# State space group in the memory and banks that the recurrence had; linear attention's states beside the recurrence

## The chip, the cores and the metric

One core of one Trainium2 chip runs the whole block. The metric is the device time of one execution, in microseconds (us). The kernel is written in a tile framework: a scheduler orders the instructions of each engine when the kernel is built, from the order of the program, the pools of memory and the banks; the order is then fixed. The engines are TensorE (PE), VectorE (DVE), ScalarE (ACT), GpSimd (POOL) and SyncE (SP, which issues nearly all DMAs).

## What is computed

One layer of a hybrid block on 1024 latent tokens with a prefix of 256 context tokens, width 1024. A normed input goes through one projection (`w_in`) into three mixers that run over the tokens in both directions; their outputs are joined and projected (`w_out`); a mixture of experts follows. The three mixers, cut to what matters here:

```python
def rwkv7_scan(r, w, k, v, a, b, s0):            # 4 heads of 64
    def step(s, inp):
        r_t, w_t, k_t, v_t, a_t, b_t = inp
        sa = jnp.einsum('bhvk,bhk->bhv', s, a_t)
        s = s * w_t[:, :, None, :] + sa[..., None] * b_t[:, :, None, :] + v_t[..., None] * k_t[:, :, None, :]
        return s, jnp.einsum('bhvk,bhk->bhv', s, r_t)
...
def ssd_chunked(x, dA, bm, cm, s0):              # 8 heads of 64, chunks of 128
    a_cs = jnp.cumsum(dA, -1)
    decay_in = jnp.exp(jnp.where(causal, a_cs[..., :, None] - a_cs[..., None, :], -jnp.inf))
    scores = jnp.einsum('bclhn,bcshn->bhcls', cm, bm) * decay_in
    y_diag = jnp.einsum('bhcls,bcshp->bclhp', scores, x)
    decay_to_end = jnp.exp(a_cs[..., -1:] - a_cs)
    states = jnp.einsum('bclhn,bhcl,bclhp->bchpn', bm, decay_to_end, x)
    ...
    y_off = jnp.einsum('bclhn,bchpn,bhcl->bclhp', cm, states[:, :-1], jnp.exp(a_cs))
    return y_diag + y_off
...
def gla_chunked(q, k, v, logg, s0):              # 4 heads, keys 32, values 64, chunks of 64
    b_cs = jnp.cumsum(logg, 2)
    att = jnp.einsum('bclhd,bcshd->bchls', q * jnp.exp(b_cs - ref), k * jnp.exp(ref - b_cs))
    o_intra = jnp.einsum('bchls,bcshe->bclhe', att, v)
    kv = jnp.einsum('bcshd,bcshe->bchde', k * jnp.exp(b_end[:, :, None] - b_cs), v)
    s_start = ...   # the running sum of kv over the chunks, decayed
    o_inter = jnp.einsum('bclhd,bchde->bclhe', q * jnp.exp(b_cs), s_start)
    return o_intra + o_inter
```

## The kernel before

The program goes through these stages. (1) To about 562 us: norm, `w_in` in column groups, the preparation of each mixer, and for the recurrence the inverse of a triangular matrix per chunk (`rw_inverse`). (2) The recurrence, in 20 steps of 64 tokens, both directions and all heads at once (`rw_step`, with `rw_out` one step behind). (3) The rest of the three mixers. (4) The output projection (`outproj`), the router, the experts.

**A step of the recurrence** (all its matmuls are 64x64, at line 596 in the helper `heads`, 16 to a group): `pa` from `cd`, `v` and the state `Z`; ACT copies it to `rh`; `pb` from `rh` and `sm`; ACT copies it to `u`; `pz` from `v`, then from `u`; DVE adds `pz` to `Zd` and gives the next `Z`; POOL makes `Zd`. `py`, the output, is summed from `cd` and `v`, `cd` and `Z`, `sm` and `u`, and ACT (p < 12) or DVE writes it to `y`. SP loads for every step `cd` (768 KB, two buffers), `sm` (line 582, and 585 from step 4 on) and two halves of `v` (line 588, three buffers). `pa`, `pb` and `pz` share the two banks `ch`, `py` has the one bank `rg`.

**GLA**: `gla_states` loads `vg`, transposes ten gate tiles (`ptg`), makes the decays (`la`, `cum`, `kend`) and sums the states (`ptk` transposes, `pkv` matmuls, `gS`); `gla_out` makes the scores (`pat`, line 881) and outputs (`po`, lines 904 and 907) in two groups, norms them (`gsq`, `pin`, `pbn`) and stores them to `mixD`.

**SSD**: `ssd_dt` makes the step sizes and their sums; each sum is split into three bfloat16 parts (`csp`), which go to `difD` in DRAM in 48 stores (lines 1056 to 1058). `ssd_states` goes through ten chunks: transposes `ptx` and `ptB`, weighting `xs` (one direction on DVE, the other on POOL), matmul `pss`, then the running sum `sacc`, `S` on POOL, stored to `stD`. `ssd_out` goes through eight tiles: `ssd_weights` builds the decay matrix `pe` from a mask and two products over `df` (lines 1135, 1137, 1139), `pa` (line 1149), `Cd` on POOL and the scores `pcb`; then `pyd` (line 1188), whose second operand `st` is a state loaded from `stD`.

`outproj_consts` splits `w_out` into `woh` and `wol` and makes small constants (`pgr`, `prb`); `outproj` makes `pso` in two halves for each of eight tiles. `rw_finish` norms the output of the recurrence (`pm`, `fs`, `pin`, `pbn`).

What sets the order: a stage can only run beside another if its pool of memory and its banks are open at the same time. Before, `ps2` (ch=2, rg=1) and `ps3` (sd=3, gl=2) are open from the recurrence to the projection, and the pools `sd` and `gl` lie on the right side, in memory that is free by then, so that the states of both GLA and SSD run beside the recurrence. The scheduler mixes them into the gaps.

## Time and profile before

| | us |
|---|---|
| three runs: median (lowest, highest) | 1535.78 (1533.09, 1540.34) |
| profiled execution | 1533.99 |
| its span, from first to last instruction | 1532.2 |
| last inverse ends, recurrence begins | about 562 to 572 |
| recurrence ends | about 738.5 |
| first pso of the projection | about 905 |
| last pso | about 1010 |
| PE busy in the span | 1340.5 (87%) |
| DVE, ACT, POOL busy | 785.2, 515.4, 389.5 |

The table gives where the stages lie in the profiled execution; busy shares of the whole span say little, since every stage has another limit. All the change's edits lie between 562 and 1010 us, but for the set-up of the fixed part of `difD`, which lies in the first stage. "SPq" in the trace is the time in which SP issues a DMA, not that of the transfer.

### The profile page before, as it was taken

To read this page: it belongs to the slowest core of one execution; us is meant where nothing else is said; L and a number is where in the kernel's file an instruction comes from. 1 tells how busy PE (TensorE), PEld (TensorE's weight loads), DVE (VectorE), ACT (ScalarE), POOL (GpSimd) and SP (SyncE) were. 2 spreads that over 40 slices of the span, in tenths; PEclk is the share of its full clock that TensorE was granted. 3 is DMA by queue.
4 is the path that set the end of the run, shared out by engine and by line. 5 is a ranking of instruction groups with operands and counts; after the bars stand their busy time and mean duration, and the time that the engine had idled before them with its cause. 6 is when DMAs were issued, how large, how long until landed. Compare 5 with 4: busy or idle time off the path is not lost. (4 is left out here: it accounts for less than half of the span.)

```text
span 1532.2 us, 28018 instructions
## 1 busy us (share of the span) xinstructions
PE 1340.5 (87%) x11077; PEld 1111.9 (73%) x11077; DVE 785.2 (51%) x1482; ACT 515.4 (34%) x1056; POOL 389.5 (25%) x432
## 2 busy tenths in 40 slices
PE   7897899999797776777889989993999999999984
PEld 3585677777676774666557767762999999999984
DVE  4849868889979854414564472227102212112532
ACT  5544334443363134422433352220212212212333
POOL 3312432343334111413453252112101111111112
PEclk9997899999899777889856589995999999999998
DMA  9454867677661467476544365425988868868984
GB/s 320 134 156 138 201 153 169 167 189 180 162 144 31 93 141 203 127 229 207 185 145 118 97 208 171 145 97 193 368 299 288 271 201 301 294 224 299 311 266 123
DMA packets 297253, 296.81 MB, mean 194 GB/s; under 512 B 114281, under 2 KB 214890, under 8 KB 297119
## 3 DMA queue, kind: packets, MB, share of 16 engines
q1 hardware_dynamic: 288095, 269.81, 57.7%
q0 software_dynamic: 7872, 20.97, 5.7%
q10 hardware_dynamic: 1152, 4.19, 0.7%
q8 instruction: 89, 1.46, 0.4%
q14 instruction: 45, 0.37, 0.1%
HBM read 221.44 MB, written 73.72 MB: 193 GB/s over the span
## 5 line engine op out<-in xcount | busy, mean ns | idle before, releaser
L1576 PE MATMUL p<-hT,w 128*128 128x144 f32 (+10 forms) x2048 | 263.2, 288 | 0.0
L1576 PEld LDWEIGHTS p<-hT,w 128*128 128x128 f32 x2048 | 257.6, 192 | 0.6
L262 PE MATMUL psi<-hlo,whi 128*128 128x512 f32 (+1 forms) x440 | 172.0, 391 | 5.0 <-DVE hlo L234 3.8
L261 PE MATMUL psi<-hhi,whi 128*128 128x512 f32 (+1 forms) x440 | 170.3, 389 | 0.0
L263 PE MATMUL psi<-hhi,wlo 128*128 128x512 f32 (+1 forms) x440 | 169.9, 387 | 0.3 <-POOL wlo L254 0.3
L1583 PE MATMUL p<-hid,w 128*128 128x144 f32 (+10 forms) x1024 | 136.6, 294 | 8.4 <-DVE hid L1578 7.2
L1583 PEld LDWEIGHTS p<-hid,w 128*128 128x128 f32 x1024 | 133.9, 199 | 9.0 <-DVE hid L1578 7.5
L1602 POOL DMA_INDIRECT acc<-yr,rows x27 | 41.4, 1532 | 323.0 <-DVE yr L1598 188.2
L1578 DVE TENSOR_TENSOR hid<-hid,p 128x144 f32<-128x144 f32 (+10 forms) x64 | 18.7, 294 | 170.0 <-PE p L1576 165.9
L262 PEld LDWEIGHTS psi<-hlo,whi 128*128 128x128 f32 x440 | 85.6, 195 | 26.0 <-DVE hlo L234 5.6
L263 PEld LDWEIGHTS psi<-hhi,wlo 128*128 128x128 f32 x440 | 85.4, 194 | 19.1 <-issue 3.4
L261 PEld LDWEIGHTS psi<-hhi,whi 128*128 128x128 f32 x440 | 85.8, 195 | 17.7 <-issue 2.1
L1598 DVE TENSOR_SCALAR yr<-pty,rows 128x512 f32<-128x512 f32 (+8 forms) x46 | 32.7, 741 | 112.4 <-PE pty L1592 105.2
L1584 ACT ACTIVATE yT<-p,mods 128x144 f32<-128x144 f32 (+10 forms) x128 | 43.0, 374 | 112.7 <-PE p L1583 112.5
L1577 ACT ACTIVATE hid<-p 128x144 f32<-128x144 f32 (+10 forms) x64 | 18.2, 284 | 168.8 <-PE p L1576 168.7
L739 DVE SCALAR_TENSOR_TENSOR co<-gr,pc,co 128x512 f32<-128x512 f32 x72 | 59.4, 849 | 6.5 <-ACT co L728 4.7
L190 DVE SCALAR_TENSOR_TENSOR aacc<-wada,csig,aacc 128x512 f32<-128x512 f32 x56 | 51.6, 921 | 15.6 <-DMA wada<-in_ada_w_dram 15.3
L262 PE MATMUL pso<-wol,mh 128*128 128x512 f32 x128 | 52.8, 412 | 3.3 <-DVE wol L1222 2.2
L261 PE MATMUL pso<-woh,mh 128*128 128x512 f32 x128 | 52.4, 412 | 1.0 <-DVE go L1265 1.0
L263 PE MATMUL pso<-woh,ml 128*128 128x512 f32 x128 | 52.6, 411 | 0.0
L463 PE MATMUL psg<-AR,BK 64*128 64x128 f32 x320 | 46.6, 304 | 4.0 <-DVE BK L456 1.6
L463 PEld LDWEIGHTS psg<-AR,BK 64*128 64x128 f32 x320 | 39.5, 204 | 13.4 <-issue 4.0
(540 smaller groups left out, 2668.3 us busy)
## 6 DMA issues: line engine op xcount, KB each, us to landing
w<-in_moe_w_dram SPq DMA_DIRECT2D x47, 2048.0 KB
wada<-in_ada_w_dram SPq DMA_DIRECT2D x32, 512.0 KB
cd<-stepD SPq DMA_DIRECT2D x20, 768.0 KB
wraw<-in_w_in_dram SPq DMA_DIRECT2D x24, 512.0 KB
aw<-in_ada_w_dram SPq DMA_DIRECT2D x10, 512.0 KB
stepD<-AR SPq DMA_DIRECT2D x40, 128.0 KB
mabD<-G SPq DMA_DIRECT2D x40, 128.0 KB
stepD<-G SPq DMA_DIRECT2D x40, 128.0 KB
```

The lines of the kernel that those rows point to most:

```text
L190: nc.vector.scalar_tensor_tensor(acc, w[:, k % 2], g.sg[:, k, 0:1], acc, op0=OP.mult, op1=OP.add)
L261: nc.tensor.matmul(ps, whi(k), xhi(k), start=k == 0, stop=False)
L262: nc.tensor.matmul(ps, whi(k), xlo(k), start=False, stop=False)
L263: nc.tensor.matmul(ps, wlo(k), xhi(k), start=False, stop=k == 7)
L463: nc.tensor.matmul(pg[h][:, c, :], bkf[HS[h], c], arf[HS[h], c], start=True, stop=True)
L739: nc.vector.scalar_tensor_tensor(o, src(dy, dx), w(3 * dy + dx), o, op0=OP.mult, op1=OP.add)
L1576: nc.tensor.matmul(p[:, 0:n], w[:, k, fs], hT[:, k, s0:s0 + n], start=k == 0, stop=k == 7)
L1578: nc.vector.tensor_mul(hid[:, f, 0:n], hid[:, f, 0:n], p3[:, 0:n])
L1583: nc.tensor.matmul(p[:, 0:n], w2[:, f, 128 * k:128 * k + 128], hid[:, f, 0:n], start=f == 0, stop=f == 3)
L1584: nc.scalar.activation(yT[:, k, 0:n], p[:, 0:n], AF.Copy, scale=g.mods[:, 40 + k, 0:1])
L1598: nc.vector.tensor_scalar(yr[0:m, h], pf, wt[0:m, b:b + 1], None, op0=OP.mult)
L1602: nc.gpsimd.indirect_dma_start(out=g.acc, out_offset=bass.IndirectOffsetOnAxis(ap=rows[0:m, 0, b:b + 1], axis=0), in_=yr[0:m, :], in_offse ...
```

## The change

It moves four things. The banks: beside the recurrence only GLA has banks of its own (gl=3), and the recurrence has ch=3 and rg=2; when it has ended, its banks become SSD's (sd=4, rg=1). The memory: `gl` and the new pool `yp` (with `y`, and the tiles of `rw_finish`) are on the right during the recurrence; SSD's pool `sd` takes the memory of `rw` on the left, so that no SSD work can start before the last step is done. The order of the program: GLA's states, the finish of the recurrence, SSD's step sizes, GLA's output, then SSD's states and output, with the projection's constants between the tiles. And the layout of `difD`: six rows of tiles instead of eight, the parts of two products stacked along the contraction (K from 36 to 48), so that the third `pe` matmul goes; the parts go to DRAM in one store (`partsD`), and 16 + 8 DMAs from there to `difD`. Tags of banks follow: `pm` and its norm to sd, `pyd` to rg, `pgr` and `prb` to gl, `pso` to sd, `pto` to gl. All eight banks are in use before (ch=2, rg=1, sd=3, gl=2), and in both new stages (ch=3, rg=2, gl=3; sd=4, rg=1, gl=3).

```diff
@@ -638,7 +638,7 @@
     if p == 4:
-        g.y = g.rw.tile([128, 2, TL], F, tag="y", name="y")
+        g.y = g.yp.tile([128, 2, TL], F, tag="y", name="y")
     py = py.rearrange("p (b d) t -> p b d t", b=2)
@@ -653,16 +653,16 @@
             ts = slice(t0, t0 + 512)
-            x = g.rw.tile([128, 1536], F, tag="cd", name="fw", bufs=2)
+            x = g.yp.tile([128, 1536], F, tag="fw", name="fw", bufs=2)
             yc, bv, gt = (x[:, 512 * i:512 * i + 512] for i in range(3))
-            sq = g.rw.tile([128, 512], F, tag="sm", name="fs", bufs=2)
+            sq = g.yp.tile([128, 512], F, tag="fs", name="fs", bufs=2)
             nc.sync.dma_start(bv, g.bvD[b, :, ts])
             nc.sync.dma_start(gt, g.gtD[b, :, ts])
-            pm = g.ps.tile([128, 512], F, tag="ch", name="pm")
+            pm = g.ps.tile([128, 512], F, tag="sd", name="pm")
             nc.tensor.matmul(pm, g.blk64, g.y[:, b, ts], start=True, stop=True)
...
             nc.scalar.activation(sq, yc, AF.Square)
-            pb = inv_norm(g, g.rw, "ch", sq, g.blk64[:, ::64], 1.0 / 64, 2)
+            pb = inv_norm(g, g.yp, "sd", sq, g.blk64[:, ::64], 1.0 / 64, 2)
             nc.vector.tensor_mul(yc, yc, pb)
@@ -949,17 +949,18 @@
     nc = g.nc
-    g.difD = g.dram.tile([8, 128, 8, 128], BF, name="difD")
-    t = g.tmp.tile([128, 8, 128], BF, tag="rv", name="dift", bufs=1)
+    g.difD = g.dram.tile([8, 128, 6, 128], BF, name="difD")
+    t = g.tmp.tile([128, 6, 128], BF, tag="rv", name="dift", bufs=1)
     nc.gpsimd.memset(t, 0.0)
...
         for h in range(4):
-            nc.sync.dma_start(t[o + 24 + 3 * h:o + 27 + 3 * h, h], g.oneb[0:3])
+            for r in (24, 36):
+                nc.sync.dma_start(t[o + r + 3 * h:o + r + 3 + 3 * h, h], g.oneb[0:3])
     nc.sync.dma_start(g.difD.rearrange("c p i t -> p c (i t)"),
-                      t.rearrange("p i t -> p (i t)")[:, None].to_broadcast([128, 8, 1024]))
+                      t.rearrange("p i t -> p (i t)")[:, None].to_broadcast([128, 8, 768]))
@@ -1048,14 +1049,17 @@
     nc.vector.tensor_scalar(parts[:, 2], parts[:, 0], -1.0, None, op0=OP.mult)
+
+    pD = g.dram.tile([3, 128, 3, 128], BF, name="partsD")
+    nc.sync.dma_start(pD.rearrange("k p i t -> p k (i t)"), parts.rearrange("p k i t -> p k (i t)"))
     for d in range(2):
...
             for h in range(4):
-                src = parts[64 * d + 4 * q + h:64 * d + 64:8]
-                o = 64 * q + 3 * h
-                nc.sync.dma_start(g.difD[:, o + 12 * d:o + 12 * d + 3, h], src[:, 0])
-                nc.sync.dma_start(g.difD[:, o + 24:o + 27, 4 + d], src[:, 2])
-                nc.sync.dma_start(g.difD[:, o + 24:o + 27, 6 + d], src[:, 1])
+                o = 64 * q + 12 * d + 3 * h
+                nc.sync.dma_start(g.difD[:, o:o + 3, h], pD[0, 64 * d + 4 * q + h:64 * d + 64:8])
+            for r, k in ((24, 2), (36, 1)):
+                nc.sync.dma_start(g.difD[:, 64 * q + r:64 * q + r + 12, 4 + d],
+                                  pD[k, 64 * d:64 * d + 64].rearrange("(c q h) i t -> q c (h i) t", q=2, h=4)[q])
@@ -1119,12 +1123,12 @@
     nc.sync.dma_start(xt, g.xsD[:, :, ts])
-    df = W.tile([128, 8, 128], BF, tag="df", name="df", bufs=2)
+    df = W.tile([128, 6, 128], BF, tag="df", name="df", bufs=2)
     nc.sync.dma_start(df, g.difD[tl - 2])
...
         nc.sync.dma_start(C2[HS[d]], g.xsD[:, 5, ts].rearrange("(g n) t -> n g t", g=2))
-    K = [slice(64 * q, 64 * q + 36) for q in range(2)]
+    K = [slice(64 * q, 64 * q + 48) for q in range(2)]
     R = [df[K[q], 0:4].rearrange("p h t -> p (h t)") for q in range(2)]
@@ -1134,9 +1138,7 @@
         for q in range(2):
-            nc.tensor.matmul(pe[q].rearrange("p h t -> p (h t)"), df[K[q], 4 + d], R[q], start=False, stop=False)
-        for q in range(2):
-            nc.tensor.matmul(pe[q].rearrange("p h t -> p (h t)"), df[K[q], 6 + d], R[q], start=False, stop=True)
+            nc.tensor.matmul(pe[q].rearrange("p h t -> p (h t)"), df[K[q], 4 + d], R[q], start=False, stop=True)
         for q in range(2):
@@ -1180,7 +1182,7 @@
         nc.gpsimd.tensor_mul(yz, xt[:, 0:4, :], g.dskip[:, :, None].to_broadcast([128, 4, 128]))
-        py = g.ps.tile([128, 4, 128], F, tag="sd", name="pyd")
+        py = g.ps.tile([128, 4, 128], F, tag="rg", name="pyd")
@@ -1209,7 +1211,7 @@
     for hf in range(2):
-        pg = g.ps.tile([128, 4, 128], F, tag="ch", name="pgr")
+        pg = g.ps.tile([128, 4, 128], F, tag="gl", name="pgr")
         for j in range(4):
@@ -1229,7 +1231,7 @@
     nc.sync.dma_start(rb[:, 4:20], dap(g.a["moe_re_b"], 0, [[0, 128], [1, 16]]))
-    pr = g.ps.tile([128, 512], F, tag="ch", name="prb")
+    pr = g.ps.tile([128, 512], F, tag="gl", name="prb")
     for k in range(8):
@@ -1258,13 +1260,13 @@
         for hf in range(2):
-            ps = g.ps.tile([128, 512], F, tag="ch", name="pso")
+            ps = g.ps.tile([128, 512], F, tag="sd", name="pso")
             h = slice(512 * hf, 512 * hf + 512)
...
             nc.gpsimd.tensor_add(x[:, h], x[:, h], go)
-            pt = g.ps.tile([128, 4, 128], F, tag="gl" if tl < 4 else "sd", name="pto")
+            pt = g.ps.tile([128, 4, 128], F, tag="gl", name="pto")
             for j in range(4):
@@ -1803,8 +1805,9 @@
     B.close("psm", "ps1")
-    B.open("left", "ps2", ch=2, rg=1)
-    B.open("right", "ps3", sd=3, gl=2)
+    B.open("right", "ps3", gl=3)
+    B.open("left", "ps2", ch=3, rg=2)
+    M.open("right", "yp", "gl")
     M.open("left", "rw")
@@ -1813,23 +1816,25 @@
     late()
-    rw_finish(g)
     M.close("rw")
-    M.open("right", "sd", "gl")
+    B.close("ps2")
+    B.open("left", "ps5", sd=4, rg=1)
+    M.open("left", "sd")
     g.vg = g.gl.tile([128, 10, 280], F, name="vg")
...
     gla_states(g)
+    rw_finish(g)
     ssd_dt(g)
+    gla_out(g)
+    M.close("gl", "yp")
+    M.open("right", "op")
     ssd_states(g)
     ssd_out(g, range(2, 6))
-    gla_out(g)
-    M.close("gl")
-    M.open("left", "op")
     outproj_consts(g)
...
     outproj(g)
-    M.close("op", "ab", "sd")
-    B.close("ps2", "ps3")
+    M.close("op", "sd", "ab")
+    B.close("ps5", "ps3")
     B.open("left", "ps4", mm=5, tp=3)
```

How the instructions of three places stand now. A number behind a name tells apart buffers of the same name; the pairs of the two halves of a head group are counted together (x8 stands for eight pairs).

PE, from `pb` of step 7 on, before; `cd_5637` is the load of step 7, `cd_5724` that of step 8:

```order
L596 MATMUL pb_5667<-rh_5665,sm_5639 64x64 x8
L596 MATMUL pz_5680<-v_5643,cd_5637 64x64 x8
L596 MATMUL py_5784<-cd_5637,Z_5655 64x64 x2
L859 MATMUL pkv_7043<-vg_6891,ke_7041 32x64 x4
L859 MATMUL pkv_7049<-vg_6891,ke_7041 32x64 x2
L596 MATMUL pz_5680<-u_5676,cd_5637 64x64 x8
L596 MATMUL pa_5733<-v_5730,cd_5724 64x64 x8
L596 MATMUL py_5784<-sm_5639,u_5676 64x64 x8
L596 MATMUL pa_5733<-Z_5742,cd_5724 64x64 x8
L859 MATMUL pkv_7049<-vg_6891,ke_7041 32x64 x2
L849 MATMUL ptk_7055<-ident_85,kend_7006 128x128
L596 MATMUL py_5871<-cd_5724,v_5730 64x64 x8
```

PE at the same place in the changed kernel, from the row ahead of `pb` of step 7 on; `cd_5651` is the load of step 7 there, `cd_5738` that of step 8:

```order
L596 MATMUL py_5885<-cd_5738,v_5744 64x64 x5
L596 MATMUL pb_5681<-rh_5679,sm_5653 64x64 x8
L596 MATMUL pz_5694<-v_5657,cd_5651 64x64 x8
L596 MATMUL pa_5747<-v_5744,cd_5738 64x64 x7
L596 MATMUL pz_5694<-u_5690,cd_5651 64x64 x8
L596 MATMUL pa_5747<-v_5744,cd_5738 64x64
L596 MATMUL py_5798<-sm_5653,u_5690 64x64 x8
L596 MATMUL py_5885<-cd_5738,v_5744 64x64 x3
L859 MATMUL pkv_6982<-vg_6798,ke_6980 32x64 x4
L859 MATMUL pkv_6988<-vg_6798,ke_6980 32x64
L596 MATMUL pa_5747<-Z_5756,cd_5738 64x64 x8
L596 MATMUL py_5885<-cd_5738,Z_5756 64x64 x8
```

Before, `cd` of the next step is first read by `pa`, behind `pz` from `u`. Now five pairs of the next step's `py` read it ahead of `pb`, and seven pairs of `pa` ahead of `pz` from `u`; so it stands in all of steps 5 to 18.

SP in the middle of the recurrence, before:

```order
L1056 DMA difD<-csp 8x3x128
L1057 DMA difD<-csp 8x3x128
L1058 DMA difD<-csp 8x3x128
L588 DMA v<-vtD 64x4x64 x2
L1056 DMA difD<-csp 8x3x128
L580 DMA cd<-stepD 128x1536
L1057 DMA difD<-csp 8x3x128
L1058 DMA difD<-csp 8x3x128
L1056 DMA difD<-csp 8x3x128
L1057 DMA difD<-csp 8x3x128
L582 DMA sm<-sD 128x2x128
L585 DMA sm<-mabD 128x2x64 x2
```

and in the changed kernel:

```order
L588 DMA v<-vtD 64x4x64 x2
L580 DMA cd<-stepD 128x1536
L582 DMA sm<-sD 128x2x128
L585 DMA sm<-mabD 128x2x64 x2
L588 DMA v<-vtD 64x4x64 x2
L580 DMA cd<-stepD 128x1536
L582 DMA sm<-sD 128x2x128
L585 DMA sm<-mabD 128x2x64 x2
```

The stores to `difD` are gone from among the loads of the steps; they now stand behind the finish of the recurrence, as one store of `partsD` and 24 DMAs.

PE at the end of the recurrence, before, where `py_6749` is the output of step 19:

```order
L1094 MATMUL pss_7640<-xs_7641,B_7638 64x256
L596 MATMUL py_6749<-cd_6681,v_6687 64x64 x8
L596 MATMUL py_6749<-cd_6681,Z_6699 64x64 x8
L596 MATMUL py_6749<-sm_6683,u_6720 64x64 x8
L849 MATMUL ptk_7247<-ident_85,kend_7214 128x128
L1094 MATMUL pss_7640<-xs_7643,B_7638 64x256
L1077 MATMUL ptx_7657<-ident_85,xt_7655 128x128 x4
L1079 MATMUL ptB_7662<-ident_85,xt_7655 128x128
L662 MATMUL pm_6780<-y_5547,blk64_91 128x512
```

and in the changed kernel, where the first `pss` rows of the second state chunk stand (those of the first chunk are spread a little ahead):

```order
L907 MATMUL po<-gq_6831,gS 64x64 x11
L907 MATMUL po<-gq_6832,gS 64x64 x16
L370 MATMUL pin<-blk_91,gsq 128x2 x4
L1098 MATMUL pss<-xs,B 64x256 x3
L1081 MATMUL ptx<-ident,xt 128x128 x4
L1083 MATMUL ptB<-ident,xt 128x128
L378 MATMUL pbn<-ident,gsq 128x128 x4
L370 MATMUL pin<-blk_91,gsq 128x2 x4
L1098 MATMUL pss<-xs,B 64x256
L1081 MATMUL ptx<-ident,xt 128x128 x4
```

SSD's state matmuls stood among the last steps of the recurrence, and stand now behind the outputs of GLA (`po`).

## Rows read from the trace of the kernel before

**Rows 1.** The page's first line.

```profile
span 1532.2 us, 28018 instructions
```

**Rows 2.** One tile's instructions: pb, records, min/median/max ns, first and last start.

```profile
L596 PE MATMUL pb<-rh,sm x320: 218/218/366, 568.6 to 735.9; 64*64 64x64 f32 x160
```

**Rows 3.** Timeline of PE at the recurrence's end: start us, us, engine, line, out<-in, records.

```profile
738.08 0.63 PE L596 MATMUL py<-sm,u 64*64 64x64 f32 x16
```

**Rows 4.** Timeline of PE at the pb of step 5.

```profile
624.87 1.12 PE L596 MATMUL pb<-rh,sm 64*64 64x64 f32 x16
```

**Rows 5.** Stretches: us, busy us of PE, PEld, DVE, ACT, POOL; clock, DMA share, GB/s.

```profile
640.00:660.00 20.00, 10.93 (x246) 9.71 (x241) 1.68 (x5) 2.49 (x9) 1.24 (x2) 0.80 0.45 128
680.00:700.00 20.00, 17.67 (x456) 15.04 (x457) 9.41 (x21) 7.12 (x19) 4.86 (x6) 1.00 0.83 245
738.50:757.00 18.50, 14.85 (x132) 8.49 (x128) 14.73 (x27) 12.80 (x20) 10.92 (x9) 1.00 0.56 177
788.00:830.00 42.00, 39.80 (x446) 30.78 (x444) 16.59 (x30) 9.62 (x19) 13.96 (x16) 0.59 0.38 112
738.50:905.00 166.50, 152.61 (x1359) 101.24 (x1355) 93.59 (x167) 71.62 (x118) 67.86 (x63) 0.68 0.49 148
905.00:925.00 20.00, 15.76 (x68) 11.72 (x66) 12.68 (x18) 7.03 (x9) 11.18 (x8) 0.91 0.30 102
```

**Rows 6.** Timeline of PE about a wait for cd; in brackets idle time ahead, releaser.

```profile
651.22 0.68 PE L596 MATMUL pz<-u,cd 64*64 64x64 f32 x16
656.90 1.12 PE L596 MATMUL pa<-v,cd 64*64 64x64 f32 x16 [5.00 <-DMA cd<-stepD]
```

**Rows 7.** Timeline of SP's queue: difD's first and last of 48 issues, two cd loads.

```profile
605.76 0.66 SPq L1056 DMA_DIRECT2D difD<-csp  x1
...
652.47 0.38 SPq L580 DMA_DIRECT2D cd<-stepD  x1
...
658.38 0.57 SPq L1058 DMA_DIRECT2D difD<-csp  x1
...
676.35 0.54 SPq L580 DMA_DIRECT2D cd<-stepD  x1
```

**Rows 8.** Timeline of PE in steps without difD stores.

```profile
673.37 0.57 PE L596 MATMUL pb<-rh,sm 64*64 64x64 f32 x14
...
675.06 0.68 PE L596 MATMUL pz<-u,cd 64*64 64x64 f32 x16
...
680.89 0.68 PE L596 MATMUL pa<-v,cd 64*64 64x64 f32 x16 [0.15 <-PE pz L596]
...
690.43 0.57 PE L596 MATMUL pb<-rh,sm 64*64 64x64 f32 x14
```

**Rows 9.** Groups by line on PE, 562 to 738.5: busy us, mean ns | idle before.

```profile
L1094 PE MATMUL pss<-xs,B 128*64 128x256 f32 x38 | 9.6, 525 | 0.8 <-DVE B L1085 0.8
...
L1077 PE MATMUL ptx<-ident,xt 128*128 128x128 f32 x24 | 5.6, 338 | 2.5 <-DMA xt<-xsD 2.5
...
L1079 PE MATMUL ptB<-ident,xt 128*128 128x128 f32 x6 | 2.1, 349 | 0.0
```

**Rows 10.** Groups by line on PE, 738.5 to 905.

```profile
L1139 PE MATMUL pe<-df 36*128 36x512 bf16 x32 | 13.7, 510 | 0.0
...
L859 PE MATMUL pkv<-vg,ke 64*32 64x64 f32 x104 | 2.6, 247 | 0.0
L849 PE MATMUL ptk<-ident,kend 128*128 128x128 f32 x7 | 2.6, 367 | 0.0
```

**Rows 11.** Groups by line on POOL, 562 to 905.

```profile
L1110 POOL TENSOR_TENSOR S<-S,sacc 128x512 f32<-128x512 f32 x8 | 11.4, 1419 | 13.1 <-DVE S L1101 13.0
L1091 POOL TENSOR_TENSOR xs<-x,wend 128x512 f32<-128x512 f32 x9 | 11.3, 1255 | 12.2 <-ACT x L1081 9.1 <-PE pss L1094 3.1
L1109 POOL TENSOR_TENSOR sacc<-S,dec 128x512 f32<-128x512 f32 x8 | 9.3, 1160 | 0.4 <-DVE S L1101 0.3
...
L1222 POOL TENSOR_TENSOR wol<-wraw,woh 128x1024 fp32r<-128x1024 f32 x1 | 2.3, 2347 | 4.3 <-ACT woh L1221 4.3
```

## Prediction

> **What bounds the kernel now.** I first read the span and then cut it into stretches. The profiled execution took 1533.99 us: a span of 1532.2 us [rows 1] and 1.8 us around it. The median of the three runs is 1535.78 us, so it stands 1.8 us above that execution. The sum is made on the profile and these 1.8 us are added at the end. A difference of 0.5% (7.7 us) is about what a measurement can tell from no change.
>
> The change touches the stretch from 568 to 1010 us. Three parts of it have three different limits. The recurrence runs from its first pb at 568.6 to its last at 735.9 [rows 2] and its last py matmul ends at about 738.6 [rows 3]; its sixth pb, step 5, starts at 624.87 [rows 4]. Steps 5 to 19 thus take 735.5 - 624.9 = 110.6 us, 7.9 us a step (735.9 is the last record of a group of 16 that starts near 735.5). It is a chain, not a load on TensorE: in 640 to 660 PE is busy 10.93 of 20 us, in 680 to 700 it is busy 17.67 of 20 [rows 5]. The reader should see where the slow steps lose their time: pz<-u ends at 651.9 and the next matmul starts at 656.90, after 5.00 us of waiting for cd [rows 6], the 768 KB of the next step. That load was issued only at 652.47, because SP was issuing difD stores without a break: 48 of them, 605.76 to 658.38, at some 0.6 us each, 29 us of SP [rows 7]. Where SP is free the step is short: pz<-u 675.06 to 675.74, cd issued 676.35, and the waiting pa follows at 680.89 without loss [rows 7, 8].
>
> From 738.5 to 905 PE is the limit: busy 152.61 of 166.5 us, at a mean granted clock of 0.68; 788 to 830 stood at 0.59, so nearly all of it at 1.2 GHz, although PE was busy 39.80 of 42 us [rows 5]. There GLA's small matmuls alternate with the SSD tiles. The output projection then begins with a stumble (905 to 925: PE 15.76 of 20 us [rows 5]).
>
> **Recurrence.** The change takes the SSD work and the 48 difD issues out of the recurrence, and gives it three banks for its chain and two for py instead of two and one. GLA's states stay beside it. At the start I expect a small loss: all matmuls of the last inverse now stand ahead of the first pa, and GLA's transposes, which wait for vg, one step earlier. I count 3 us (between 0 and 8) until step 5.
>
> Then SP is free, and by the rows of 673 to 681 one would expect steps of less than 6 us. The new order forbids that. In each of steps 5 to 18, part of py of step p+1 now stands ahead of pb of step p, so cd of step p+1 must have landed before pb(p) starts, not only before pa(p+1). Its buffer (cd still has two) is freed by pz<-u(p-1). A step is then a closed ring: 0.3 us from the end of pz<-u to the issue, 4.4 us of load (652.47 to 656.90 [rows 6, 7]), 0.4 us for the five py pairs, and from pb to the end of pz<-u 2.4 us (673.37 to 675.74 [rows 8]). This gives 7.5 us; with some of the steps at the low clock I take 7.6. So 14 steps take 106 us against 110.6: -4.5. With the 3 us at the start and half a microsecond of changed tail the recurrence ends 1 to 2 us earlier: **-1.5 us**. Bounds: -31 (5.7 us a step, as three steps from 673.37 to 690.43 show [rows 8]: 2.2 x 14) and +24 (below).
>
> The 48 stores become one store of the parts, 24 DMAs of rows, and a way through DRAM. They are issued after the recurrence, beside the rest of GLA's output: 25 issues at 0.6 us, 15 us of SP against some 55 us of PE work that covers them; cost 0. If the cover failed, the first pe of tile 2 would be up to 15 us late. The Trainium skill, "DMA: Bandwidth & Descriptors", section "Issuing engines are not separate DMA queues", says that the time a sequencer takes to initiate a DMA is usually small beside the DMA. The rows show otherwise for stores of 6 KB: the queue that they filled held back a load for which PE waited 5.00 us [rows 6, 7]. By the rule, freeing SP would leave the steps at 7.9 us, and the sum below would come to 1531.3 instead of 1526.8; I go by the rows.
>
> The eight more small loads of the fixed difD part are in the prelude, at most 8 x 0.6 us of SP there, hidden under projections that keep PE; 0, at most +2.
>
> **From the end of the recurrence to the projection.** PE must do 152.61 us, as before, and besides:
> the SSD state chunks that ran beside the recurrence, pss 9.6, ptx 5.6 and ptB 2.1: +17.3 [rows 9];
> less the third pe matmul, 13.7 [rows 10], which K = 48 saves; records of pipelined matmuls overlap, so I take -11;
> less GLA's state tail, pkv and ptk, 2.6 + 2.6 [rows 10], which now ends inside the recurrence: -5;
> plus some 2 us of matmuls that now come ahead of the projection instead of inside it.
> That is 156 us. With the idle time of before, 13.9 us, it makes 170. The order takes GLA's output apart from the SSD tiles; where SSD work stands alone the clock was 1.00 at 738.5 to 757 even with PE only 14.85 of 18.5 us busy [rows 5], so I take 5 us off for a better clock: 165, that is **-1.5 us**. Bounds: -16 and +17 (both rivals below).
>
> POOL has to carry the state chain in one piece now: xs, sacc and S cost 1.26, 1.16 and 1.42 us a chunk [rows 11], 9 chunks 35 us, and four wol subtractions of 2.35 us [rows 11] lie between: 44 us. PE has matmuls for that time: 26 us of the nine chunks (17.3 for six), pgr and prb of the projection's constants, and pe, pa and pcb of the first tiles. I count no exposed wait beyond the idle time above.
>
> **Projection.** w_out is split into woh and wol among the state chunks, and pso has four banks instead of two. The 4.2 us that PE idles in 905 to 925 go, and about 2 us of matmuls that ran at the low clock there: **-6 us** (between -8 and 0). What follows to 1532 is untouched.
>
> **Sum.** -1.5 - 1.5 - 6 = -9: 1525 on the profile, **1526.8 us** against the median, 0.6% faster.
>
> **Rivals.**
> *The recurrence really is freed.* If loads land sooner than 4.4 us because the DMA queues are emptier, the ring opens and the steps come to 5.7 us: 1.9 x 14 = 27 us less than in my sum, some 1500. For it: the DMA share is 0.83 in the good steps [rows 5], with SSD traffic among it that goes away. Against: 4.43 us was measured at a share of 0.45 [rows 5, 6, 7], where nothing crowded it. Chance 0.13.
>
> *The recurrence falls to the low clock (slower).* With the SSD matmuls gone PE idles about 3 us in every ring, at the cd wait. At the low clock the 16 records of pa take 1.12 us instead of 0.68 [rows 6, 8], right behind the 5.00 us wait. All PE work on the ring (0.4 + 2.4) grows by 1.65 to 4.6 us, and the ring from 7.5 to 9.3 us; that is 1.7 x 14 = 24 us over my sum, some 1551. It decides from 8.8 us a step on (1.2 x 14 = 17 us, which brings it to 1544). Against: 640 to 660 held a clock of 0.80 with PE idle almost half of the time [rows 5]. Chance 0.17. The Trainium skill, "TensorE: Matmul & The Clock Gate", section "Loop structure matters more than you think", speaks against this change in the same way: a DMA wait between groups of matmuls lets TensorE go cold, and the next group runs cold. The trace agrees at one place, the pa of 1.12 us behind the wait; the mean of 0.80 shows that it does not hold for the whole of such a stretch.
>
> *The states hang on POOL and DVE (slower).* The last tile's state closes the chain that tile 2's output needs, through a store and a load. If PE runs out of other work the states take the pace at which four chunks came between 739 and 764, 6.2 us each, 56 us instead of 44, and a store and load of some 5 us: +17, about 1544. For it: DVE was busy 14.73 of 18.5 us in that stretch [rows 5]. It decides if PE idles more than 20 us between the end of GLA's output and the first pyd. Chance 0.15.
>
> *SSD output at the full clock.* Its 56 us of PE work (a third of the stretch) lay mostly in the clock of 0.6; at 1.0 they shrink by a quarter, 14 us: some 1512. Chance 0.10.
>
> **How the numbers follow.** My sum has a chance of 0.45, with 1513 to 1540 as its own range. More than half of that lies below 1528.1, a little over a third within 0.5%. With the faster rivals (0.13, 0.10) "faster" comes to 0.47; "same" to 0.23, part of it from the POOL rival; "slower" to 0.30, from the two slow rivals and the upper end of mine. The range, 1497 to 1553, reaches to the free recurrence below and the cold one above.
>
> **What would show it.** Right: in the profile of the changed kernel pb(5) at 625 to 632, steps of 7.3 to 8 us with a wait for cd ahead of py in nearly each, no difD issue before the last py; pss only from some 50 us after the last py on; the first pso 163 to 167 us after it; then 100 us to the end of the projection with no idle PE at its start. Wrong: steps under 6 us or over 9; a granted clock above 0.8 or below 0.6 in the stretch ahead of the projection; PE idle among the state chunks for over 20 us; or a changed length of what lies before 562 or behind the projection.

## The result, and the profile after

The change makes the kernel slower: a median of 1590.95 us (1585.79 to 1600.95, four runs) against 1538.06 us for the kernel before in the same sessions; the ratio is 1.0345 with an interval of 1.027 to 1.0421. That is 53 us more, where 9 us less was forecast; it lies beyond the range. The profiled execution took 1600.95 us, the longest of the four, and its span is (the page's first line and its engines):

```profile
span 1599.1 us, 27952 instructions
...
PE 1364.1 (85%) x11045; PEld 1130.8 (71%) x11045; DVE 782.8 (49%) x1482; ACT 508.0 (32%) x1049; POOL 390.6 (24%) x432
```

PE is busy 24 us more than before in a span 67 us longer, so 43 us of the loss is idle time of PE. (In the second profile of the same kernel, below, it is 5 us and 54 us: the waiting repeats, most of the added busy time does not.) Where it lies shows in the stages of the two profiled executions, each from the first and last start of a tile's matmuls (us):

| | first pb | first to last pb | last pb to first pso | pso | behind the last pso | span |
|---|---|---|---|---|---|---|
| before | 568.6 | 167.3 | 169.8 | 122.7 | 503.8 | 1532.2 |
| changed | 581.2 | 171.6 | 223.3 | 116.2 | 506.8 | 1599.1 |
| difference | +12.6 | +4.3 | +53.5 | -6.5 | +3.0 | +66.9 |

In the changed kernel the recurrence's pb (one tile's instructions) answers to [rows 2], and the pb of step 5 (timeline of PE) to [rows 4]:

```profile
L596 PE MATMUL pb<-rh,sm x320: 218/282/366, 581.2 to 752.8; 64*64 64x64 f32 x160
```

```profile
635.99 0.24 PE L596 MATMUL pb<-rh,sm 64*64 64x64 f32 x1
```

Steps 5 to 19 take 752.3 - 636.0 = 116.3 us, 8.3 us a step, where 7.6 was forecast and 7.9 was before. The stretches of the changed kernel, with the columns of [rows 5] (us, busy us of PE, PEld, DVE, ACT, POOL, clock, DMA share, GB/s):

```profile
581.20:754.50 173.30, 122.18 (x2642) 107.01 (x2642) 47.98 (x104) 49.98 (x122) 31.16 (x34) 0.79 0.50 148
754.50:805.00 50.50, 45.58 (x519) 36.87 (x520) 32.65 (x93) 17.88 (x34) 8.30 (x9) 0.58 0.29 89
805.00:875.00 70.00, 57.30 (x417) 37.74 (x413) 37.18 (x74) 23.19 (x39) 29.47 (x23) 0.67 0.60 188
875.00:902.00 27.00, 12.63 (x34) 4.17 (x35) 8.52 (x8) 8.57 (x14) 21.46 (x15) 0.50 0.49 158
902.00:976.00 74.00, 64.18 (x349) 38.66 (x350) 36.89 (x48) 29.84 (x49) 30.53 (x32) 0.55 0.45 129
976.00:1092.30 116.30, 116.30 (x560) 88.71 (x559) 29.15 (x52) 23.41 (x41) 19.32 (x15) 0.98 0.38 132
754.50:976.00 221.50, 179.69 (x1311) 117.44 (x1311) 115.24 (x221) 79.48 (x134) 89.76 (x79) 0.59 0.46 142
```

The reader should set the last line beside the 166.50 us line of [rows 5]: PE is busy 180 us instead of 153, and idle 42 us instead of 14. In 902 to 976, the state space output alone, the clock is 0.55, so nearly all at 1.2 GHz, though PE is busy 64 of 74 us. That is not the same in every execution: in the second profile of this kernel the same stretch (900.7 to 965.9) took 65 us at a clock of 0.74.

The ring that the prediction worked out stands in the timeline of PE:

```profile
657.25 0.22 PE L596 MATMUL pa<-v,cd 64*64 64x64 f32 x1
...
659.67 0.33 PE L849 MATMUL ptk<-ident,kend 128*128 128x128 f32 x1
662.09 0.47 PE L596 MATMUL py<-cd,v 64*64 64x64 f32 x9 [2.09 <-DMA cd<-stepD]
...
662.45 0.57 PE L596 MATMUL pb<-rh,sm 64*64 64x64 f32 x14
...
664.26 0.22 PE L596 MATMUL pa<-v,cd 64*64 64x64 f32 x1
...
669.61 0.47 PE L596 MATMUL py<-cd,v 64*64 64x64 f32 x9 [2.55 <-DMA cd<-stepD]
...
669.98 0.57 PE L596 MATMUL pb<-rh,sm 64*64 64x64 f32 x14
```

and of SP's queue:

```profile
657.48 0.34 SPq L580 DMA_DIRECT2D cd<-stepD  x1
...
664.87 0.54 SPq L580 DMA_DIRECT2D cd<-stepD  x1
```

pz from u has ended and cd is issued at 657.48; it lands at 662.09, 4.6 us later, and the py pairs that waited for it stand right ahead of pb. From one landing to the next it is 7.5 us (662.09 to 669.61), as forecast, where the clock is full. Not every round is like it. The load for step 12 is issued at 680.03 (SP's queue), and PE goes on at 686.41, 6.4 us later:

```profile
680.03 0.54 SPq L580 DMA_DIRECT2D cd<-stepD  x1
```

```profile
686.41 0.77 PE L596 MATMUL py<-cd,v 64*64 64x64 f32 x9 [4.19 <-DMA cd<-stepD]
```

Over the thirteen rounds from step 6 on, in which PE waits for cd, the load takes 4.3 to 6.4 us, 5.0 on average (forecast 4.4), and from pb to the end of pz from u it is 2.1 to 3.8 us, 3.0 on average (forecast 2.4); such a round takes 8.6 us. Over the recurrence PE waits for cd (waits, 562 to 780: total, times, longest):

```profile
PE py L596 <- DMA cd<-stepD: 33.1, 14, 4.2
```

against 13.9 us in five waits before, at pa.

Behind the recurrence the longest wait of PE is for the first state of an output tile (waits of PE, 754.5 to 976, and the timeline of PE around it):

```profile
PE pyd L1190 <- DMA st<-stD: 12.2, 1, 12.2
PE pin L370 <- POOL sqs L1196: 6.9, 3, 3.1
PE pss L1098 <- DVE xs L1095: 5.6, 3, 2.4
```

```profile
889.21 0.58 PE L1151 MATMUL pa<-df,dirs 48*128 48x512 bf16 x1 [0.50 <-ACT E L1143]
901.94 0.69 PE L1190 MATMUL pyd<-Cd,st 128*64 128x128 f32 x4 [12.16 <-DMA st<-stD]
```

The timeline of POOL shows what was late. The last pss ends at 873.3, but the running sums S end only at 897.3; Cd and yz of the first tiles and wol subtractions stand among them in POOL's order. From there to 901.9 it is the store of the state and its load:

```profile
885.09 2.94 POOL L1155 TENSOR_TENSOR Cd<-Cd,C 128x512 f32<-128x512 f32 x2
887.99 1.26 POOL L1114 TENSOR_TENSOR S<-S,sacc 128x512 f32<-128x512 f32 x1
889.21 1.04 POOL L1184 TENSOR_TENSOR yz<-xt,dskip 128x512 f32<-128x512 f32 x1
890.21 2.34 POOL L1224 TENSOR_TENSOR wol<-wraw,woh 128x1024 fp32r<-128x1024 f32 x1
892.50 1.04 POOL L1113 TENSOR_TENSOR sacc<-S,dec 128x512 f32<-128x512 f32 x1
893.62 1.26 POOL L1114 TENSOR_TENSOR S<-S,sacc 128x512 f32<-128x512 f32 x1
894.96 1.04 POOL L1113 TENSOR_TENSOR sacc<-S,dec 128x512 f32<-128x512 f32 x1
896.08 1.26 POOL L1114 TENSOR_TENSOR S<-S,sacc 128x512 f32<-128x512 f32 x1
```

### The profile page after: what moved, and what is told of

It is laid out like the page before. It is cut to its first block, busy times and chain, and to the rows that moved or that the text cites. A ratio compares the mean times of both kernels' runs of the same rounds, so it can differ in the third digit from the quotient of the medians.

```text
span 1599.1 us, 27952 instructions
## 1 busy us (share of the span) xinstructions
PE 1364.1 (85%) x11045; PEld 1130.8 (71%) x11045; DVE 782.8 (49%) x1482; ACT 508.0 (32%) x1049; POOL 390.6 (24%) x432
## 5 line engine op out<-in xcount | busy, mean ns | idle before, releaser
L615 DVE TENSOR_TENSOR Z<-Zd,pz 128x256 f32<-128x256 f32 x18 | 7.5, 419 | 90.8 <-PE pz L596 90.8
```

## The experiments

All times below are medians; "against before" is the ratio to the kernel before, run on the same chip, with its interval.

**The changed kernel again**, no edit.

> The changed kernel itself, once more, beside the others on the same chip. Its first profiled execution was the slowest of its four runs, and its first 560 us were 7 us longer than before. Theory: that is scatter between executions; here 1586 to 1595 us, and the inverses' last matmul within 3 us of that of the kernel before. Rival: the change costs the first stage 5 to 8 us each time (its extra small loads), and the last px comes again 5 us or more later than before.

1592.66 us, 1.0368 (1.0304 to 1.0433). The stages repeat: first pb 578.7, recurrence 171.3 between its pb, 215.9 us from there to the first pso, 115.8 us of pso, span 1586.6. Behind the recurrence the result's profiled execution, at 223.3 us, was 7 us longer than this one. Its stretch there, columns as above, to be set beside the last line of the table:

```profile
752.00:965.90 213.90, 168.61 (x1311) 112.00 (x1312) 115.20 (x220) 79.43 (x134) 90.48 (x79) 0.64 0.47 147
```

PE is idle 45 us here and 42 there, and its wait for st is 12.3 us and 12.2; PE's busy time is 11 us less, at a clock of 0.64 instead of 0.59. So the idle time repeats, and a part of the added busy time belongs to the one execution. The last px comes 4 us later than before (572.3 against 568.5), between the 3 us of the theory and the 5 us of the rival; see below.

### The recurrence

**A third cd buffer.**

```diff
-    cd = T.tile([128, 1536], F, tag="cd", name="cd", bufs=2)
+    cd = T.tile([128, 1536], F, tag="cd", name="cd", bufs=3)
```

> The changed kernel with a third buffer for cd, nothing else: a load can be issued one step earlier, so that the ring of load, py, pb, pz is open. Theory (the ring sets the step): steps 5 to 19 fall from 8.3 us to 6.0 to 6.8 us, PE's wait for cd (33 us there) nearly goes, and the time falls by 20 to 30 us against the changed kernel, to 1560 to 1570. Rival (the chain over ACT, DVE and PE at the low clock sets it, and the wait for cd only stands where another would): steps stay at 7.8 or more, and the time falls by less than 8 us.

1553.96 us, 1.0081 (1.0051 to 1.011): 39 us less than the changed kernel. pb now runs

```profile
L596 PE MATMUL pb<-rh,sm x320: 212/218/366, 579.7 to 701.9; 64*64 64x64 f32 x160
```

122 us instead of 171; steps 5 to 19 take 701.5 - 628.1 = 73.4 us, 5.2 us a step, less than expected. The wait for cd is gone from PE's longest ones, and with it the low clock of these steps. Steps 5 to 19 in the changed kernel and with the third buffer, columns as above:

```profile
635.99:752.29 116.30, 83.58 (x2019) 76.87 (x2014) 27.42 (x70) 23.50 (x68) 16.42 (x21) 0.84 0.50 146
```

```profile
628.09:701.48 73.39, 63.36 (x1930) 59.25 (x1928) 19.08 (x52) 18.75 (x57) 12.58 (x17) 1.00 0.76 224
```

What follows the recurrence grew by 16 us (215.9 to 232.3), so part is given back there.

**One py bank.**

```diff
-    B.open("left", "ps2", ch=3, rg=2)
+    B.open("left", "ps2", ch=3, rg=1)
```

> The changed kernel with one bank for py in the recurrence instead of two (ch=3, rg=1, gl=3; one bank lies idle), cd still in two buffers. py of the next step can then not run ahead of pb, and cd of the next step is first read by pa, behind pz from v. Theory (it is the second py bank that let the order read cd too early and closed the ring): the ring has the load, one group of pa and one of pz, about 6.3 us; PE's wait for cd falls below 20 us, steps 5 to 19 come to 6.3 to 7.3 us, and the time falls by 12 to 25 us against the changed kernel, to 1567 to 1580. Rival (only a third buffer helps; or one bank makes py wait for its copy to y): steps of 8 us or more, and within 6 us of the changed kernel.

1560.9 us, 1.0152 (1.0094 to 1.0209): 32 us less, more than expected. pb runs from 574.7 to 726.8, 152.1 us; steps 5 to 19 take 726.3 - 624.5 = 101.8 us, 7.3 us a step, and PE's wait for cd, now again at pa, is

```profile
PE pa L596 <- DMA cd<-stepD: 17.6, 11, 4.1
```

So the second bank, given to loosen the recurrence, is what closed the ring: it let the scheduler put py of the next step ahead of pb. Taking the bank away makes the ring shorter, and a third buffer takes it away. Of the 30 us between the profile of the changed kernel run again and this one (spans 1586.6 and 1556.2), 19 lie in the recurrence, 8 behind it and 4 ahead of it, where pa stands among the last px again.

**The third buffer in the kernel before**, the same edit and the same for `fw`, which shares the tag.

> The kernel before with a third buffer for cd alone. Theory (SP is busy with the 48 difD stores, which hold back the load whatever buffers there are; the new layout is what frees it): within 8 us of the kernel before, 1530 to 1546. Rival (the buffer is worth as much here as with the new difD layout, where it gave 13 us, or as in the changed kernel, where it gave 39): 1527 or less.

1517.68 us, 0.9846 (0.9796 to 0.9897): 24 us faster than the kernel before. The theory falls. The wait for cd in [rows 6] was put down to SP alone, and a third buffer takes it away although the 48 stores stay: pb runs 148.4 us instead of 167.3, and no wait for cd is left there. With three buffers the load can be issued a step earlier (that of step 9 at 648.68, while its first reader, pa, starts at 659.12), so an issue that waits behind stores no longer reaches PE.

### What the parts are worth

**The new difD layout alone**, the hunks of `ssd_consts2`, `ssd_dt` and `ssd_weights` put on the kernel before.

> The kernel before with the new difD layout alone: K = 48, two pe matmuls, one store of the parts and 24 DMAs from DRAM, the eight extra loads at the start. Banks, memory and program order of before. Theory: this part is a gain, 11 us of PE in the late stretch and some 15 us of SP issues in the recurrence; 1524 to 1533 us. And if it is the eight small loads that lengthen the first stage, its last px comes 3 to 6 us later than before here too. Rival: the way through DRAM and the small loads eat it up, 1537 to 1545.

1521.12 us, 0.9879 (0.984 to 0.9917): 18 us faster, more than expected. pb runs 156.3 us (-11), and from the last pb to the first pso it is 157.5 us (-12). The last px comes at 568.6, as before: the eight small loads cost nothing that this profile shows.

**The new order of the program alone**, in the banks and memory of before:

```diff
     late()
-    rw_finish(g)
-    M.close("rw")
     M.open("right", "sd", "gl")
...
     gla_states(g)
+    rw_finish(g)
+    M.close("rw")
     ssd_dt(g)
-    ssd_states(g)
-    ssd_out(g, range(2, 6))
     gla_out(g)
...
     M.open("left", "op")
+    ssd_states(g)
+    ssd_out(g, range(2, 6))
     outproj_consts(g)
```

> The kernel before with the new order of the program alone (states of linear attention, finish of the recurrence, step sizes, output of linear attention, then the state space states and output), in the banks and the memory of before, so that the state space states can still run beside the recurrence. Theory (what costs is that the state chunks lost their cover): within 8 us of the kernel before, 1532 to 1548. Rival (the new order, linear attention's output in one piece ahead of the state space output, costs by itself at the low clock): 1560 or more.

1538.25 us, 0.999 (0.9959 to 1.0022): no difference, as the theory had it. The scheduler still puts the state chunks beside the recurrence, since their banks and memory are open.

So two parts of the change give -18 us and 0 us, and the whole +53. If parts simply add up, what is left, the banks and the memory, costs some 71 us; below it is measured with a third buffer, and is less there.

**difD and third buffer on the kernel before**, and the same **with the new order**; all but the banks and the memory.

> The kernel before with the new difD layout and a third buffer for cd, nothing else. Theory (in the recurrence a late cd load is what costs most, in either kernel, and the state space states hide beside it): the recurrence falls from 167 us between its first and last pb to 140 to 150, and the time to 1505 to 1520. Rival (with the states beside it the recurrence is bound by ACT, DVE and PE's order, not by cd): 158 us or more between those pb, and 1525 or more.

> The kernel before with the new difD layout, the third cd buffer and the new order of the program, in the banks and memory of before: all that the change does but for its banks and memory, and the buffer. Theory (the order of the program is worth nothing by itself): within 8 us of the same kernel without the new order, 1500 to 1516. Rival (linear attention's output in one piece leaves the state space output together at a better clock): 1498 or less.

1507.84 us, 0.9785 (0.9745 to 0.9824), and 1507.45 us, 0.9786 (0.9737 to 0.9834). These are the fastest kernels of the study, 32 to 34 us under the kernel before in the same sessions and 83 us under the changed one. The first did not get there as expected: its pb still run 168.5 us, and all ten state chunks now lie beside them (the last pss at 688.3, in the kernel before 763.5). The gain lies behind. Its two stretches, columns as above:

```profile
570.00:740.50 170.50, 138.02 (x2719) 108.25 (x2719) 80.04 (x168) 69.69 (x161) 68.39 (x65) 0.83 0.74 222
740.50:873.30 132.80, 118.43 (x1216) 87.14 (x1217) 74.68 (x137) 58.01 (x96) 45.75 (x46) 0.66 0.44 132
```

and those of the changed kernel with a third buffer:

```profile
579.70:704.00 124.30, 102.00 (x2520) 88.84 (x2522) 38.42 (x85) 45.38 (x110) 26.30 (x30) 0.84 0.65 193
704.00:934.20 230.20, 181.73 (x1442) 115.58 (x1438) 126.66 (x240) 84.61 (x147) 93.53 (x84) 0.60 0.46 140
```

This pair is the study's main reading. With a third buffer in both, the recurrence takes 124 us without the state space group and 170 us with its step sizes, all its state chunks and the weights of two of its eight output tiles (8 of the 32 pe) in it; the work behind it takes 230 us and 133 us. Beside the recurrence this work costs 46 us, behind it 97. The two profiles differ by 56 us in all (spans 1560.9 and 1504.8): +97 behind the recurrence, -46 in it, +10 ahead of it, -11 in the projection and +6 behind that; between the medians it is 46 us (1553.96 and 1507.84). The pair changes the banks and the memory as a whole, so the 46 and the 97 us hold all that comes with them, not the chunks' matmuls alone; and some of the projection's constants stand ahead of the first pso in one kernel and behind it in the other. This pair differs in the order of the program too. The kernel with the new order differs from the changed kernel with a third buffer in the banks and the memory alone, and says the same:

```profile
576.70:745.10 168.40, 134.51 (x2719) 105.78 (x2719) 79.96 (x168) 69.95 (x161) 68.37 (x65) 0.86 0.75 225
745.10:871.00 125.90, 115.68 (x1225) 85.71 (x1225) 72.66 (x147) 56.97 (x94) 44.37 (x44) 0.69 0.45 132
```

That is 44 us beside the recurrence and 104 behind it, and between the medians (1553.96 and 1507.45) the banks and the memory cost 46 us where cd has three buffers.

### Behind the recurrence

**wol on DVE.**

```diff
-        (nc.gpsimd if k % 2 else nc.vector).tensor_sub(g.wol[:, k, :], w, g.woh[:, k, :].bitcast(F))
+        nc.vector.tensor_sub(g.wol[:, k, :], w, g.woh[:, k, :].bitcast(F))
```

> The changed kernel with all eight wol subtractions on DVE instead of four on POOL, nothing else. They stand in POOL's order among the last running sums of the state space group. Theory (POOL's chain sets when the last states land): 9 to 10 us of POOL go, PE's wait of 12 us for st shrinks to 2 to 5 us, and the time falls by 7 to 10 us against the changed kernel, to 1581 to 1584. Rival (DVE is the other half of the state chain, and takes it up): the wait stays over 9 us and the time within 3 us of the changed kernel.

1582.05 us, 1.0312 (1.0245 to 1.0379); the wait for st is 9.2 us instead of 12.2. The time is as the theory has it, but the interval overlaps that of the changed kernel, and part of the difference between the profiles lies in the recurrence, which the edit does not touch. The sums S end 22 us behind the last pss instead of 24. Inconclusive.

**Two banks for pyd** (`sd=3, rg=2` in `ps5`).

> The changed kernel with the banks after the recurrence cut as sd=3, rg=2 instead of sd=4, rg=1: pyd has two banks, the weights and pso three. Theory (PE in the state space output is bound by its own work at the low clock, not by the one pyd bank): within 4 us of the changed kernel. Rival (one bank for pyd makes the tiles wait for one another, and that keeps the clock down): the stretch from the first pyd with a state to the first pso falls from 74 us to 65 or less, and the time by 8 us or more.

1590.01 us, 1.0316 (1.0241 to 1.0391): no difference that can be told. The stretch from the first pyd with a state to the first pso is 71.5 us; in the two profiles of the changed kernel it is 74 and 65, so it varies more than a second bank could be seen to give. That the one pyd bank costs 8 us or more is not borne out.

**The chunks' own work left out.** `ssd_states` without ptB, xs, pss and the copies to S, the states cleared.

> The changed kernel with the weighting, the matmul and the copies of every state chunk left out, and the states set to zero instead (transposes, x, the running sums and their stores and loads stay). Theory (behind the recurrence a state chunk is a chain over ACT, DVE, POOL and PE that nothing covers): the 71 us between the first pss and the last fall by 40 us or more, and the time by 40 to 55 us against the changed kernel, to 1537 to 1552. Rival (only its PE work counts, some 25 us of records at the low clock): the time falls by 15 to 28 us, to 1564 to 1577.

1573.88 us, 1.0219 (1.016 to 1.0279): 19 us less, as the rival had it; from the last pb to the first pso it is 190.5 us instead of 215.9. But in this run another wait came up, for the loads of the chunks (waits of PE, 560 to 1000):

```profile
PE ptx L1085 <- DMA xt<-xsD: 14.9, 6, 8.8
```

**Four xt buffers** (`bufs=4` at both tiles with the tag `xt2`).

> The changed kernel with four buffers instead of two for the xt tiles of the state space group: four loads now stand in SP's queue ahead of the 24 DMAs to difD, before there were two (and a third behind the first transposes). Theory (SP's 16 us of difD issues hold back the loads of the third and later state chunks, for which ACT and POOL wait 17.5 us): that wait falls below 5 us, the last pss comes 8 to 16 us earlier after the end of the recurrence, and the time falls by 8 to 16 us against the changed kernel, to 1577 to 1585. Rival (the chunks stand behind linear attention's output on PE anyway): within 4 us of it.

1593.59 us, 1.0349 (1.0268 to 1.0429): nothing. In the trace SP still issues the 24 difD DMAs from 805 to 821, now with five chunk loads ahead of them instead of three, and pss runs from 803.1 to 867.7, almost as in the changed kernel (805.4 to 872.7). The theory falls: PE's order has the rest of the first chunk's pss, and the second chunk, behind linear attention's second group anyway, whose last po starts at 816.6 here and at 818.9 in the changed kernel.

**One py bank, wol on DVE and four xt buffers together**, and the same **with the chunks' own work left out**.

> The changed kernel with one py bank in the recurrence, wol on DVE and four xt buffers together. Theory (three separate costs in three places): 32 + 10 + 8 to 16 us less than the changed kernel, 1533 to 1543, which is the time of the kernel before. Rival (what is saved at one place is waited for at the next): 1548 or more.

> The kernel mend with the weighting, matmul and copies of every state chunk left out and the states set to zero, as in the run nost. Theory (with the queue out of the way, the chunks' own chain is what remains exposed behind the recurrence): 28 us or more below mend. Rival (only their PE work counts): 15 to 22 us below mend, as from the changed kernel.

1565.83 us, 1.0161 (1.0082 to 1.0239): the costs do not add up. It is no better than one py bank alone; wol and xt gave nothing beside it. Without the chunks' own work it is 1537.92 us, 0.998 (0.9944 to 1.0015): 28 us less, at the very edge of the theory. The stretch behind the recurrence with it and without it:

```profile
730.50:942.20 211.70, 170.25 (x1330) 109.68 (x1329) 129.72 (x227) 78.78 (x135) 83.82 (x75) 0.65 0.49 149
```

```profile
729.20:906.00 176.80, 143.70 (x1247) 101.59 (x1247) 113.88 (x202) 73.24 (x126) 70.12 (x66) 0.64 0.60 178
```

PE's busy time falls by 27 us, its idle time by 8.

**All three of the first edits** (third buffer, wol on DVE, two pyd banks).

> The changed kernel with all three edits of the first runs: cd in three buffers, wol on DVE, sd=3 and rg=2. Theory: they lie in different places and add up, 39 + 10 + 3 us, to 1538 to 1544. Rival: the state chunks stay exposed behind the recurrence, and what the shorter recurrence gave goes into waits there: 1548 or more.

1548.0 us, 1.0043 (1.0013 to 1.0073), at the edge of the rival: 45 us under the changed kernel, of which the buffer gives 39. From the last pb to the first pso it still takes 224.2 us. Mended in this way the changed kernel is only as fast as the kernel before, within a per cent.

## Why the prediction was wrong

**The recurrence: the mechanism was right, its terms too small.** The ring was read out of the order and sized at 7.5 us; it is 7.5 us where the load takes 4.6 us and the clock is full. The step that failed here is the sum of the ring, 0.3 + 4.4 + 0.4 + 2.4, with "with some of the steps at the low clock I take 7.6": the rounds took 8.6 us, half a microsecond more from the load (5.0 us on average) and half from the matmuls on the ring (3.0 us, at a clock of 0.84 over steps 5 to 19), and a step 8.3. The rival of the low clock had 9.3. What the prediction didn't see is that the ring was the thing to undo: one buffer gives back 39 us. That is not to say that the ring makes 39 of the 53 us: between its pb the recurrence is only 4 us longer than before, and the kernel before lost time to cd too (24 us come back there by the same buffer). By comparing with the 7.9 us of a recurrence that had the state chunks in it, the sum booked a small gain for a recurrence that, free, takes 5.2 us a step. The rival "really is freed" priced this at 5.7 us, and asked for earlier landing loads; a buffer does it.

**The start** was taken as 3 us, at most 8, until step 5; the first pb is 10 to 13 us later, and pb of step 5 11 us (6.3 us from pa behind all px, the rest in the first stage, where the instructions of each engine stand in the same order as with the new difD layout alone). Over all profiles the last px of the first product lies between 566.6 and 573.3 in kernels with the banks of before and between 571.3 and 578.3 in the others; the cause of that stays open.

**Behind the recurrence: the steps that failed are "with the idle time of before, 13.9 us" and, for POOL's 44 us of state chain, "I count no exposed wait beyond the idle time above".** They counted what PE does, as if the state chunks were only matmuls that fill gaps. The forecast for the stretch was 165 us: 156 busy, 13.9 idle, 5 off for the clock. Measured were 221.5 us, 180 busy and 42 idle, and in the second profile 213.9 us, 169 busy and 45 idle. So the exposed waits alone are 28 to 31 us over the forecast, and they repeat; PE's work is 13 to 24 us over it, and more so where the clock is lower. The clock was 0.59 and 0.64 instead of 0.68, so "5 us off for a better clock" had the wrong sign, and matmuls became dearer (pyd 412 ns on average, before 372; pss 539 where [rows 9] has 525):

```profile
L1098 PE MATMUL pss<-xs,B 128*64 128x256 f32 x72 | 21.6, 539 | 7.4 <-DVE xs L1095 5.6 <-POOL xs L1095 1.7
L1190 PE MATMUL pyd<-E,x 128*64 128x128 f32 x128 | 21.5, 412 | 1.1 <-DVE E L1161 1.1
```

The idle time is the wait of 12.2 us for st; 12.7 us of the 70 from 805 to 875, among the chunks; 9.8 us in 902 to 976, where the output tiles stand alone; and smaller pieces. The POOL rival, with a chance of 0.15, was right by its own sign: from the last po (818.9) to the first pyd with a state (901.9) PE idles 27 us, over the 20 it asked for. It priced that at 17 us; the stretch came out three times as far over the forecast. The pair of stretches above gives the cause its size: work that cost 46 us beside the recurrence costs 97 behind it. How these 97 us divide is settled only in part: leaving out the chunks' own weighting, matmuls and copies gives 19 and 28 us between the medians, and 25 and 35 us of the stretch from the last pb to the first pso; the rest (transposes, running sums, their stores and loads, the step sizes, the banks themselves, and waits that moved from one to another when one was taken away) was not separated.

**The cover of the difD issues** (cost 0) held in the changed kernel: they run 16 us on SP, mostly beside linear attention's output. Moving loads ahead of them changed nothing.

**The layout's gain** was booked as 11 us of PE; alone it gives 18 us, also in the recurrence.

**The projection** was right, and for the reason given: -6 forecast, -6.5 measured, with PE busy throughout at a clock of 0.98, and nearly the same in every kernel with the new banks there (114.8 to 116.2 us).

**The clock rule** of the Trainium skill, "TensorE: Matmul & The Clock Gate", "Loop structure matters more than you think", speaks of waits for a DMA between groups of matmuls. In the recurrence the trace agrees: over steps 5 to 19 the clock is 0.84 with the ring, in which PE waits 1.2 to 4.2 us for cd in nearly every step, and 1.00 with the third buffer, which takes the waits away. In 902 to 976 it is no such wait: PE was busy 64 of 74 us at 0.55. What holds the clock down there, and why the same stretch of the same kernel had 0.74 in another execution, no run here shows.

## What to carry to other kernels

Work that fills the gaps of a latency-bound loop can be far cheaper there than behind it (here 46 us against 97): price its removal by its whole chain over all engines, not by the busy time of the engine that is busiest. Before giving a loop more banks, look at what the scheduler does with them: a bank that lets a later step's read move up can close a ring with a buffer that is still double, and a third buffer for the streamed operand is then worth more than the bank. Take a change apart before judging it: here one part gave -18 us, one nothing, and the rest cost 46 us with a third buffer and, by subtraction, 71 without. And profile a kernel twice before reading a clock out of one execution.

## What had not been expected

A third buffer for a 768 KB load is worth 24 us in the kernel before, 13 on top of the new difD layout and 39 in the changed kernel: it depends on what stands ahead of the issue and how early the order reads the data. And PE can stand at 1.2 GHz for most of 74 us while it is busy for 64 of them (0.55 in 902 to 976), in a stretch mostly of 128x64, 48x128 and 64x128 weights, where the 128x128 matmuls of the projection that follows run at 0.98; another execution of the same kernel had 0.74 there.
